# DRAM block sums shared out between the gate products and attention's first ten heads, with a new order in the opening and in attention's fill

## The chip, the cores and the metric

The kernel runs on one NeuronCore of a Trainium2 chip. The metric is the device time of one execution in microseconds (us). A NeuronCore has five engines that work side by side: TensorE (PE in the profile, with the loads of its stationary operand shown as PEld), VectorE (DVE), ScalarE (ACT), GpSimd (POOL) and SyncE (SP). Each works through its own instructions strictly in the order in which they were written, and waits where an operand isn't there yet. Data moves between DRAM and the on-chip memory by DMA; here three engines issue transfers: SP most of the loads, ACT the stores of results, POOL the transfers that add into their target.

## The reference, cut to what matters

One layer of a bidirectional encoder on 512 tokens of width 2048, all in float32:

```
h = rmsnorm(x) * norm_w
u = h @ w_in        # gate z | x,B,C | dt fwd | dt bwd | q-compress | kv-compress + rope key | attention gate | two branch gates
dt = softplus(dt + bias);  a = -exp(a_log);  da = dt * a
y = ssd(forward) + ssd(backward) + d_skip * x;  y = grouped rmsnorm(y * silu(z))
q, k, v from the compressed parts, rope on 64 of 192 columns, 16 heads
o = softmax(q k^T * scale) v * silu(attention gate)
out = rmsnorm(x + (sigmoid(g1) * (y @ w_proj_ssm) + sigmoid(g2) * (o @ w_proj_attn)) @ w_out)
```

## The kernel before, in words

**Numbers.** Every float32 product is made of three matmuls: each operand is split into a high part `h` and a rest `l` (32-bit words that TensorE takes at one column a step), and the product is wh·xh + wh·xl + wl·xh. A weight block comes by DMA into a raw buffer (`wraw`, three of them), ACT casts it to `wh` (L163, L433), DVE subtracts to get `wl` (L164, L434); `wh` and `wl` have three buffers each.

**Stages, in order of time.**

- *Opening.* `x` is loaded in eight blocks of 128 tokens by 1024 columns, ACT squares and sums each (L210), DVE and ACT make the reciprocal root (L185 to L191), `x` is scaled (L218 on ACT, L220 on DVE), TensorE transposes it (L225) and ACT and DVE write the parts `h_h` and `h_l` (L229, L230). The first product, `dtp` (dt and the rope key), starts after the last transpose. Its two weight blocks are split with the subtraction on POOL, all later ones on DVE.
- *x, B, C of group 0* (`xbc`), with the sums of h that later products need (L758 to L778) and softplus of dt (`dt_make`, L282 to L302) on DVE beside it.
- *Gates.* Three products of 2048 x 2048 by a Strassen scheme with seven smaller ones (P1, P5, P6, P2, P3, P7, P4), for each of two column halves `cp`; each small one is four blocks of weights, 48 matmuls. During P1 and P3 a second weight block is added onto the first by DMA on POOL's queue (`w_more`, L506), four times each, for use in the next product.
- *SSD.* Four groups of scans, with `xbc`, `qkv` and `za` products as fill between the steps.
- *Attention.* 16 heads. Per head four tiles of scores, softmax on DVE and ACT, transposes (L1348) and the product with v. Between them stand parts of the products that later heads need: rope queries (`t`), values (`vp`, L1265), queries and keys (`qp`, `kp`), taken from a queue called `fill` at the rate `unit` (L1494). `fill.until` forces what a head needs just before it.
- *Two output projections* (`wps`, `wpa`, again Strassen) *and the last one* (`wo`).

**Sums in DRAM.** For `wps` and `wpa` the added blocks T1 and T3 are made ahead in DRAM: 32 copies of 512 KB (L485) and 32 transfers that add to them (L486), all on POOL's queue, ordered so that each add comes two jobs after its copy. `in_background(n)` issues the next n of them. In the kernel before it is called once per head, behind the softmax of the second tile: four jobs in each of heads 0 to 7, six from head 8 until the 64 are used up.

**What sets the order.** TensorE's order is that of the program text. On the other engines a scheduler orders the instructions by its own estimates; `tc.high_priority(offset)` pulls what it encloses forward, and `keep_in_program_order` pins an instruction.

Of the kernel before, what the change touches and what calls it, by code (L numbers as in the profile page):

```python
# [18 lines left out]
P = 128  # L19
D = 2048  # L20
# [52 lines left out]
def build(tc, a):  # L73
# [83 lines left out]
    def wchunk(src, n):  # L157
        with tc.high_priority(offset=ahead[0]):
            raw = wp.tile([P, 1024], F32, tag="wraw", bufs=3, name="wraw")[:, :n]
            nc.sync.dma_start(raw, src)  # L160
            h = wp.tile([P, 1024], F32R, tag="wh", bufs=3, name="wh")[:, :n]
            l = wp.tile([P, 1024], F32R, tag="wl", bufs=3, name="wl")[:, :n]
            act.copy(h, raw)  # L163
            (dve if ahead[0] else pool).tensor_sub(l, raw, h.bitcast(F32))  # L164
        return h, l
# [37 lines left out]
    for t in range(TT):  # L203
        xt = xp.tile([P, D], F32, name=f"xt{t}")
        ss = few(2)
        for i in range(2):
            cs = slice(i * D // 2, (i + 1) * D // 2)
            nc.sync.dma_start(xt[:, cs], a["x"][t * P:(t + 1) * P, cs])
            scr = xp.tile([P, D // 2], F32, tag="scr", bufs=1, name="scr")
            act.activation(scr, xt[:, cs], AF.Square, accum_out=ss[:, i:i + 1])  # L210
        v = few(1)
        dve.tensor_add(v, ss[:, 0:1], ss[:, 1:2])
        dve.tensor_scalar(v, v, 1.0 / D, EPS, ALU.mult, ALU.add)
        r = small_rsqrt(v, 1, lambda n: few(1))
        for i in range(2):
            cs = slice(i * D // 2, (i + 1) * D // 2)
            if t >= TT - 2 and i == 1:
                act.activation(xt[:, cs], xt[:, cs], AF.Copy, scale=r)  # L218
            else:
                dve.tensor_scalar_mul(xt[:, cs], xt[:, cs], r)  # L220
        xs_t.append(xt)
    tps = [mm(), mm(), mm(), pa(), pa(), pb(), pb(), pc()]

    def x_turn(k, t):
        pe.transpose(tps[k % 8][:, t * P:(t + 1) * P], xs_t[t][:, k * P:(k + 1) * P], ident)  # L225

    def x_out(k):
        nw = vec[:, V_NORM + k:V_NORM + k + 1]
        act.activation(h_h[:, k, :], tps[k % 8], AF.Copy, scale=nw)  # L229
        dve.scalar_tensor_tensor(h_l[:, k, :], tps[k % 8], nw, h_h[:, k, :].bitcast(F32), ALU.mult, ALU.subtract)  # L230
# [12 lines left out]
    close_pool("xp")

    def win(tile_i):
        return [(a["wi"][tile_i, 0], 0, 8), (a["wi"][tile_i, 1], 8, 8)]

    def in_gemm(tile_i, n="mm"):
        return gemm(mm(n), win(tile_i), h_h, h_l)


# [17 lines left out]

    dtp = in_gemm(T_DT, "dtp")  # L270
    ahead[0] = AHEAD
    da_d = dr.tile([64, SEQ], F32, name="da_d")
    dv_, dt64 = sxd("dv_"), sxd("dt64")
    act.activation(dv_[0:64, :], dtp[0:64, :], AF.Identity, bias=vec[0:64, V_DTB:V_DTB + 1])
    act.copy(dv_[64:128, :], dtp[64:128, :])
    put(kr_d, dv_[64:128, :])

    def dt_make(new):

        v = dv_[0:64, :]  # L280
        e, u, pl, da64 = (new(n)[0:64, :] for n in ("e", "u", "pl", "da64"))
        dve.scalar_tensor_tensor(e, v, -1.0, v, ALU.mult, ALU.min)  # L282
        act.activation(e, e, AF.Exp)
        an = few(1)[0:64, :]
        tc.keep_in_program_order(act.activation(an, vec[0:64, V_ALOG:V_ALOG + 1], AF.Exp))
# [9 lines left out]
        dve.scalar_tensor_tensor(dt64[0:64, :], pl, 2.0, v, ALU.mult, ALU.add)  # L295
        dve.tensor_scalar_mul(an, an, -1.0)
        dve.tensor_scalar_mul(da64, dt64[0:64, :], an)
        act.copy(dt64[64:128, :], da64)
        act.dma_start(da_d[0:NH, :], da64[0:NH, :])
        chunked = lambda t: t[NH:64, :].rearrange("p (c l) -> p c l", c=TT)  # L300
        dve.tensor_mul(chunked(pl), chunked(dt64)[:, :, ::-1], an[NH:64, :].unsqueeze(2).broadcast_to([NH, TT, P]))
        act.dma_start(da_d[NH:64, :], pl[NH:64, :])  # L302
        put(dt_d, dt64)

# [96 lines left out]
    def za_gen(i):  # L401
        p_ = mm("za")
        yield from gemm_steps(p_, win(T_ZA + i), h_h, h_l)
        g_ = st("za")
        act.activation(g_, p_, AF.Silu)
        put(za_d[i], g_)
# [464 lines left out]
    vneg = few(8)  # L871
    dve.tensor_scalar_mul(vneg, vec[:, V_SN + 8:V_SN + 16], -1.0)

# [377 lines left out]
    def v_gen(hg):  # L1251

        v_h = at.tile([P, TT, SEQ], F32R, tag="v_h", bufs=2, name="v_h")
        v_l = at.tile([P, TT, SEQ], F32R, tag="v_l", bufs=2, name="v_l")
        vs[hg] = (v_h, v_l)
        for i in range(2):
            wh, wl = wchunk(a["wv"][hg, i], 1024)
            for t2 in range(2):
                vp = mm("vp")
                for t in (2 * t2, 2 * t2 + 1):  # L1260
                    o = vp[:, (t % 2) * 256:(t % 2 + 1) * 256]
                    tk = slice(t * P, (t + 1) * P)
                    for k in range(4):
                        s_ = slice(k * 256, (k + 1) * 256)
                        pe.matmul(o, ckv_h[:, k, tk], wh[:, s_], start=(k == 0), stop=False)  # L1265
                        pe.matmul(o, ckv_h[:, k, tk], wl[:, s_], start=False, stop=False)
                        pe.matmul(o, ckv_l[:, k, tk], wh[:, s_], start=False, stop=(k == 3))
                        yield 1.5
                vv = vp.rearrange("p (t c) -> p t c", t=2)
                sl = (slice(None), slice(2 * t2, 2 * t2 + 2), slice(i * 256, (i + 1) * 256))  # L1270
                act.copy(v_h[sl], vv)
                dve.tensor_sub(v_l[sl], vv, v_h[sl].bitcast(F32))
            yield None

# [30 lines left out]
    rv = chain(rope_gen(0), v_gen(0))  # L1305
    for i in range(4):
        fill.add("rv", part(rv))
    fill.add(("qk", 0), qk_gen(0))
    for hd in range(1, AH):
        fill.add(("qk", hd), qk_gen(hd))  # L1310
        if hd % 4 == 1 and hd < 12:
            rv = chain(rope_gen(hd // 4 + 1), v_gen(hd // 4 + 1))
        if hd < 12 and hd % 4:
            for _ in range(2 if hd % 4 == 3 else 1):
                fill.add(("rv", hd), part(rv))
    fill.until(("qk", 0))
# [5 lines left out]
    def scores(hd, t):  # L1322
# [433 lines left out]
def layout(inp):  # L1756
# [4 lines left out]
    for g in range(GROUPS):  # L1761
# [14 lines left out]
    wk = c(ukv[:, :, :, :P].transpose(2, 1, 0, 3))  # L1776
    wv = c(ukv[:, :, :, P:].reshape(4, P, 4, 2, 256).transpose(2, 3, 1, 0, 4))
    f = np.float32
# [6 lines left out]
        np.concatenate([inp["dt_bias_fwd"][0], inp["dt_bias_bwd"][0], z64])[:, None],  # L1785
        np.concatenate([inp["a_log_fwd"][0], inp["a_log_bwd"][0], z64])[:, None]], axis=1)
    i = np.arange(P)
# [25 lines left out]
```

## Time and profile before

| what | us |
|---|---|
| median of three runs | 2008.22 (2007.54 to 2011.87) |
| the profiled execution | 2010.63 |
| its span, first to last instruction | 2008.8 |
| PE busy | 1941.0 |
| DVE busy | 1481.6 |
| ACT busy | 1032.3 |
| POOL busy | 250.1 |

The profiled execution's own time is 1.8 us above its span and 2.4 us above the median of the runs. A line of groups reads: line, engine, operation, output<-inputs, shapes, count, then busy time and the mean of one in ns, then the idle time before them and what ended it. A matmul's duration in such a line runs until its results have left the array, so successive ones overlap; how often one starts is read from the start times in the timeline. The line of a window gives its bounds, its length, busy time (and count) of each engine, the share of full clock that TensorE was granted (PEclk), the share of time in which the DMA engines were busy, and GB/s.

### The profile page before, as it was taken

The page shows a single profiled execution, that of the slowest core. Times are in us where ns is not written, and L with a number is a line of the kernel's source. Part 1 is how long each engine was busy: PE and PEld are TensorE (multiplying, and loading weights), DVE is VectorE, ACT ScalarE, POOL GpSimd, SP SyncE. Part 2 cuts the span into 40 slices and gives each one's busy share as a digit, 9 for nine tenths or more (in the row PEclk, how much of TensorE's full clock was granted, in tenths as well). Part 3 has the DMA queues.
Part 4 walks back from the last instruction along what each step waited for, and adds up shares of the span by engine and source line. Part 5 has one row for each costly group of instructions (what it writes and reads, how often), then busy time and mean ns, then how long its engine had stood idle before and what let it go on. Part 6 is the DMA issues. An engine that isn't in the chain of part 4 may idle for free.

```text
span 2008.8 us, 24843 instructions
## 1 busy us (share of the span) xinstructions
PE 1941.0 (97%) x9026; PEld 1606.9 (80%) x9026; DVE 1481.6 (74%) x2064; ACT 1032.3 (51%) x1527; POOL 250.1 (12%) x315
## 2 busy tenths in 40 slices
PE   6999999999999999999999999999979999999997
PEld 4888888888878878887878788888867787888886
DVE  7976676676659879798794767666666898879466
ACT  6444445444464757757666344444444455444243
POOL 0001001001012020120200101112112111100011
PEclk9999999999999999999999999999989999999998
DMA  5468558558444635665454956877998687857446
GB/s 189 163 192 215 152 131 220 139 134 226 130 153 142 194 122 164 213 187 181 151 173 137 271 153 177 223 202 220 236 254 297 213 290 283 277 169 242 163 88 158
DMA packets 168907, 382.78 MB, mean 191 GB/s; under 512 B 16272, under 2 KB 65552, under 8 KB 168592
## 3 DMA queue, kind: packets, MB, share of 16 engines
q1 hardware_dynamic: 103248, 233.61, 35.3%
q0 software_dynamic: 30656, 103.30, 23.3%
q10 hardware_dynamic: 34880, 44.28, 6.2%
q8 instruction: 71, 1.16, 0.2%
q14 instruction: 52, 0.43, 0.1%
HBM read 329.22 MB, written 98.04 MB: 213 GB/s over the span
## 4 chain that ended last, share of the span: by engine, by line
PE 75%; DVE 10%; DMA 8%; issue 3%; ACT 3%; POOL 0%; SPq 0%; ACTq 0%; DVEq 0%; POOLq 0%
PE P L580 11%; PE P L581 11%; PE P L579 11%; PE xbc L168 3%; PE xbc L169 3%; PE xbc L170 3%; DMA wraw<-wps 2%; PE za L170 2%; PE za L168 2%; PE za L169 2%; PE qkv L168 1%; PE qkv L170 1%; PE qkv L169 1%; PE f L1582 1%; PE f L1581 1%
## 5 line engine op out<-in xcount | busy, mean ns | idle before, releaser
L433 ACT CAST wh<-X 128x1024 fp32r<-128x1024 f32 x164 | 172.9, 1056 | 198.4 <-PE P L581 152.2
L434 DVE TENSOR_TENSOR wl<-X,wh 128x1024 fp32r<-128x1024 f32 x164 | 200.1, 1224 | 91.2 <-ACT wh L433 90.8
L164 DVE TENSOR_TENSOR wl<-wraw,wh 128x1024 fp32r<-128x1024 f32 (+2 forms) x148 | 172.6, 1167 | 91.6 <-ACT wh L163 86.1
L163 ACT CAST wh<-wraw 128x1024 fp32r<-128x1024 f32 (+2 forms) x150 | 145.1, 970 | 120.3 <-PE xbc L169 37.7
L434 DVE TENSOR_TENSOR wl<-Y,wh 128x1024 fp32r<-128x1024 f32 x88 | 107.6, 1224 | 69.7 <-ACT wh L433 69.6
L168 PE MATMUL xbc<-h_h,wh 128*128 128x512 f32 x384 | 153.3, 399 | 0.0
L433 ACT CAST wh<-Y 128x1024 fp32r<-128x1024 f32 x88 | 92.8, 1056 | 115.9 <-PE P L581 105.8
L170 PE MATMUL xbc<-h_h,wl 128*128 128x512 f32 x384 | 150.3, 391 | 0.0
L169 PE MATMUL xbc<-h_l,wh 128*128 128x512 f32 x384 | 150.1, 391 | 0.0
L579 PE MATMUL P<-wh,h_h 128*128 128x512 f32 x384 | 149.4, 389 | 0.0
L580 PE MATMUL P<-wl,h_h 128*128 128x512 f32 x384 | 149.4, 389 | 0.0
L581 PE MATMUL P<-wh,h_l 128*128 128x512 f32 x384 | 149.4, 389 | 0.0
L433 ACT CAST wh<-wraw 128x1024 fp32r<-128x1024 f32 x68 | 71.8, 1055 | 120.4 <-PE P L581 63.5
L434 DVE TENSOR_TENSOR wl<-wraw,wh 128x1024 fp32r<-128x1024 f32 x68 | 83.2, 1224 | 66.5 <-ACT wh L433 66.5
L580 PE MATMUL P<-wl,S 128*128 128x512 f32 x288 | 112.3, 390 | 0.5 <-DVE wl L434 0.5
L579 PE MATMUL P<-wh,S 128*128 128x512 f32 x288 | 112.1, 389 | 0.0
L581 PE MATMUL P<-wh,S 128*128 128x512 f32 x288 | 112.1, 389 | 0.0
L170 PE MATMUL za<-h_h,wl 128*128 128x512 f32 x256 | 100.1, 391 | 2.0 <-DVE wl L164 2.0
L168 PE MATMUL za<-h_h,wh 128*128 128x512 f32 x256 | 101.6, 397 | 0.0
L169 PE MATMUL za<-h_l,wh 128*128 128x512 f32 x256 | 99.7, 389 | 0.0
L1335 ACT ACTIVATE pr<-s,nm 128x512 f32<-128x512 f32 x64 | 44.2, 690 | 82.9 <-DVE nm L1333 82.2
L170 PEld LDWEIGHTS xbc<-h_h,wl 128*128 128x128 f32 x384 | 72.3, 188 | 15.6
(748 smaller groups left out, 5188.6 us busy)
## 6 DMA issues: line engine op xcount, KB each, us to landing
wraw<-wi SPq DMA_DIRECT2D x102, 512.0 KB, 3.7
da<-da_d SPq DMA_DIRECT2D x64, 256.0 KB, 4.1
T_wps<-wps POOLq DMA_DIRECT2D x32, 512.0 KB, 9.5
T_wpa<-wpa POOLq DMA_DIRECT2D x32, 512.0 KB, 11.4
wraw<-wps SPq DMA_DIRECT2D x24, 512.0 KB, 6.7
wraw<-wo SPq DMA_DIRECT2D x20, 512.0 KB, 3.5
xbc_d<-xbc ACTq DMA_DIRECT2D x24, 256.0 KB, 2.3
wraw<-wun SPq DMA_DIRECT2D x16, 384.0 KB, 6.1
```

The costliest lines, as they stand in the source:

```text
L163: act.copy(h, raw)
L164: (dve if ahead[0] else pool).tensor_sub(l, raw, h.bitcast(F32))
L168: pe.matmul(out, wh, xh, start=start, stop=False)
L169: pe.matmul(out, wh, xl, start=False, stop=False)
L170: pe.matmul(out, wl, xh, start=False, stop=stop)
L433: i = act.copy(hi_, raw)
L434: dve.tensor_sub(lo_, raw, hi_.bitcast(F32))
L579: pe.matmul(bs[i], xh, wh, start=(j == 0), stop=False)
L580: pe.matmul(bs[i], xh, wl, start=False, stop=False)
L581: pe.matmul(bs[i], xl, wh, start=False, stop=(j == 7))
L1335: act.activation(pr, s, AF.Exp, bias=nm, scale=SCALE, accum_out=sm_)
L1581: pe.matmul(acc, mh, wl, start=False, stop=False)
```

## The change

In words:

- *Opening.* `x`'s last block comes in two halves of 512 columns; `vec` and most of `cst` are loaded behind `x`, and from SP. The root is taken by ACT straight from the accumulated squares (the earlier parts come in as its bias), and DVE's refinement has one instruction less. The scaling of the third token block moves from ACT to DVE. Both blocks of dt weights are subtracted on DVE. Seven banks, not eight, turn in the transposes; the eighth belongs to `dtp` from the start, whose matmuls stand between the transposes, seven steps behind.
- *dt.* Softplus runs on 128 partitions by 256 columns where it had 64 by 512; the second half of the tokens is moved to the upper partitions by a DMA. There are eight stores where there were three.
- *Gates.* Each of the six halves calls `in_background(2)` after P1 and after P3: 24 jobs. Attention then has 40 left, four in each of heads 0 to 9, and none later.
- *Values.* `v_gen` multiplies all 512 columns at once where it had 256 (the weights are laid out anew for it): 192 matmuls for 384. Both weight blocks are split before the first of them.
- *Attention's fill.* `unit` is 2.95 (was 2.77), falling to 2.4 and 1.7 near the end; the forced part now counts against what is owed; rope and value parts stand at other heads.
- *za.* The SiLU that empties a `za` bank has priority.

**Where instructions move.** POOL's queue in the gates, `wz` first (X and Y are the adds of `w_more`, T the sums in DRAM). Before:

```order
L506 DMA X<-wz 128x1024 x4
L506 DMA Y<-wz 128x1024 x4
L506 DMA X<-wz 128x1024 x4
L506 DMA Y<-wz 128x1024 x4
L506 DMA X<-wgs 128x1024 x4
L506 DMA Y<-wgs 128x1024 x4
```

With the change:

```order
L530 DMA X<-wz 128x1024 x4
L509 DMA T_wps_199<-wps 128x1024 x2
L530 DMA Y<-wz 128x1024 x4
L509 DMA T_wps_199<-wps 128x1024
L510 DMA T_wps_199<-wps 128x1024
L530 DMA X<-wz 128x1024 x4
L509 DMA T_wps_199<-wps 128x1024
L510 DMA T_wps_199<-wps 128x1024
L530 DMA Y<-wz 128x1024 x4
```

Two jobs stand behind each set of four adds and ahead of the next set.

ACT at the end of the opening, from the seventh block of squares on (`xt_288` and `xt_284` are the last token block). Before:

```order
L210 ACTIVATE scr,small<-xt_288 128x1024
L218 ACTIVATE xt_271<-xt_271,small 128x1024
L210 ACTIVATE scr,small<-xt_288 128x1024
L163 CAST wh<-wraw 128x1024
L185 ACTIVATE small<-small 128x1
L163 CAST wh<-wraw 128x1024
L218 ACTIVATE xt_288<-xt_288,small 128x1024
```

With the change:

```order
L209 ACTIVATE scr,small<-xt_284 128x1024
L209 ACTIVATE scr,small<-xt_284 128x512 x2
L215 ACTIVATE small<-small 128x1
L223 ACTIVATE xt_284<-xt_284,small 128x1024
L162 CAST wh<-wraw 128x1024
L239 ACTIVATE h_h<-mm,vec 128x512 x3
```

The casts of the weights have moved behind the root, and the scaling of another token block is gone from between the squares.

PE at the start of head 8, from the last matmuls of its keys (`kp`) to its first scores (`s`). Before:

```order
L168 MATMUL kp<-ckv_h,wh 128x512
L169 MATMUL kp<-ckv_l,wh 128x512
L170 MATMUL kp<-ckv_h,wl 128x512
L1326 MATMUL s<-kh,qh 128x512
L1327 MATMUL s<-kl,qh 128x512
```

With the change, around the same scores (the last `kp` of this head stands 101 rows earlier):

```order
L167 MATMUL qp<-cq_h,wh 128x512
L168 MATMUL qp<-cq_l,wh 128x512
L169 MATMUL qp<-cq_h,wl 128x512
L1348 MATMUL s<-kh,qh 128x512
L1349 MATMUL s<-kl,qh 128x512
```

Before, the scores follow the keys at once (heads 8 and 12; ten matmuls lie between in head 4); now at least 24 matmuls and transposes lie between in every head.

The diff, cut to its core:

```diff
-    act.dma_start(cst, a["cst"])
-    act.dma_start(vec, a["vec"])
+    act.dma_start(cst[:, :P], a["cst"][:, :P])
...
             act.copy(h, raw)
-            (dve if ahead[0] else pool).tensor_sub(l, raw, h.bitcast(F32))
+            dve.tensor_sub(l, raw, h.bitcast(F32))
...
+        edges = (0, 1024, 2048) if t < TT - 1 else (0, 1024, 1536, 2048)
+        for i, cs in enumerate(slice(*e) for e in zip(edges, edges[1:])):
             nc.sync.dma_start(xt[:, cs], a["x"][t * P:(t + 1) * P, cs])
...
+        act.activation(root, ss[:, i:i + 1], AF.Sqrt, bias=most, scale=1.0 / D)
+        dve.tensor_scalar(v, ss[:, i:i + 1], 1.0 / D, most, ALU.mult, ALU.add)
+        dve.reciprocal(r, root)
+        dve.scalar_tensor_tensor(root, r, r, v, ALU.mult, ALU.mult)
+        dve.tensor_scalar(root, root, -0.5, 1.5, ALU.mult, ALU.add)
+        dve.tensor_mul(r, r, root)
...
+    BANKS = (mm, mm, mm, pa, pa, pb, pb)
+    dtp, dt_w = pc("dtp"), []
+    def dt_mm(k):
+        h, l = dt_w[k // 8]
+        cs = slice(k % 8 * P, (k % 8 + 1) * P)
+        mm3(dtp, h[:, cs], l[:, cs], h_h[:, k, :], h_l[:, k, :], k == 0, k == KT - 1)
...
+    for k in range(7, KT):
+        for t in range(TT):
+            x_turn(k, t)
+        x_out(k)
+        if k == 10:
+            dt_w.append(wchunk(a["wi"][T_DT, 1], 1024))
+        dt_mm(k - 7)
+    for k in range(KT - 7, KT):
+        dt_mm(k)
...
-        v = dv_[0:64, :]
-        e, u, pl, da64 = (new(n)[0:64, :] for n in ("e", "u", "pl", "da64"))
+        v, dt2 = vd[:, 0:HS], vd[:, HS:SEQ]
+        e, u, pl, da2 = (new(n)[:, 0:HS] for n in ("e", "u", "pl", "da2"))
...
-        act.activation(g_, p_, AF.Silu)
+        with tc.high_priority(offset=ahead[0]):
+            act.activation(g_, p_, AF.Silu)
         put(za_d[i], g_)
...
+    for g_ in gates:
+        for cp in range(2):
+            for name in ("P1", "P3"):
+                g_.hooks.setdefault((cp, name), []).append(lambda: in_background(2))
...
-        for i in range(2):
-            wh, wl = wchunk(a["wv"][hg, i], 1024)
...
+        ws = [wchunk(a["wv"][hg, i], 1024) for i in range(2)]
+        for t in range(TT):
+            vp = mm("vp")
+            for k in range(4):
+                wh, wl = (w[:, k % 2 * SEQ:(k % 2 + 1) * SEQ] for w in ws[k // 2])
+                pe.matmul(vp, ckv_h[:, k, tk], wh, start=(k == 0), stop=False)
+                pe.matmul(vp, ckv_h[:, k, tk], wl, start=False, stop=False)
+                pe.matmul(vp, ckv_l[:, k, tk], wh, start=False, stop=(k == 3))
...
-            in_background(4 if hd < 8 else 6)
+            in_background(4)
...
-        fill.until(("qk", hd))
-        unit = 2.77 if hd < AH - 2 else 2
+        while ("qk", hd) not in fill.done:
+            owed[0] -= fill.step()
+        unit = 2.95 if hd < AH - 5 else 2.4 if hd < AH - 3 else 1.7 if hd < AH - 2 else 2
```

More of the change, by code (lines that the diff above doesn't have):

```diff
@@ L204, in build @@
         xt = xp.tile([P, D], F32, name=f"xt{t}")
-        ss = few(2)
-        for i in range(2):
-            cs = slice(i * D // 2, (i + 1) * D // 2)
+        edges = (0, 1024, 2048) if t < TT - 1 else (0, 1024, 1536, 2048)
+        ss = few(3)
+        for i, cs in enumerate(slice(*e) for e in zip(edges, edges[1:])):
             nc.sync.dma_start(xt[:, cs], a["x"][t * P:(t + 1) * P, cs])
-            scr = xp.tile([P, D // 2], F32, tag="scr", bufs=1, name="scr")
+            scr = xp.tile([P, D // 2], F32, tag="scr", bufs=1, name="scr")[:, :cs.stop - cs.start]
@@ L210, in build @@
             act.activation(scr, xt[:, cs], AF.Square, accum_out=ss[:, i:i + 1])
[L211 to L220, printed above, removed]
+            if i == 0:
+                most, v, root, r = (few(1) for _ in range(4))
+                dve.tensor_scalar(most, ss[:, 0:1], 1.0 / D, EPS, ALU.mult, ALU.add)
+            elif i < len(edges) - 2:
+                dve.tensor_scalar(most, ss[:, i:i + 1], 1.0 / D, most, ALU.mult, ALU.add)
@@ new lines, in build @@
+        act.activation(root, ss[:, i:i + 1], AF.Sqrt, bias=most, scale=1.0 / D)
[4 more added lines that the diff above has]
+        dve.tensor_mul(r, r, root)
+        dve.tensor_scalar_mul(xt[:, 0:1024], xt[:, 0:1024], r)
+        if t == TT - 1:
+            act.activation(xt[:, 1024:], xt[:, 1024:], AF.Copy, scale=r)
+        else:
+            dve.tensor_scalar_mul(xt[:, 1024:], xt[:, 1024:], r)
@@ L221, in build @@
         xs_t.append(xt)
-    tps = [mm(), mm(), mm(), pa(), pa(), pb(), pb(), pc()]
+    nc.sync.dma_start(vec, a["vec"])
+    BANKS = (mm, mm, mm, pa, pa, pb, pb)
+    tps = {}
     def x_turn(k, t):
-        pe.transpose(tps[k % 8][:, t * P:(t + 1) * P], xs_t[t][:, k * P:(k + 1) * P], ident)
+        if k not in tps:
+            tps[k] = BANKS[k % 7]()
+        pe.transpose(tps[k][:, t * P:(t + 1) * P], xs_t[t][:, k * P:(k + 1) * P], ident)
     def x_out(k):
         nw = vec[:, V_NORM + k:V_NORM + k + 1]
-        act.activation(h_h[:, k, :], tps[k % 8], AF.Copy, scale=nw)
-        dve.scalar_tensor_tensor(h_l[:, k, :], tps[k % 8], nw, h_h[:, k, :].bitcast(F32), ALU.mult, ALU.subtract)
+        act.activation(h_h[:, k, :], tps[k], AF.Copy, scale=nw)
+        dve.scalar_tensor_tensor(h_l[:, k, :], tps[k], nw, h_h[:, k, :].bitcast(F32), ALU.mult, ALU.subtract)
@@ L232, in build @@
+    dtp, dt_w = pc("dtp"), []
[3 more added lines that the diff above has]
+        mm3(dtp, h[:, cs], l[:, cs], h_h[:, k, :], h_l[:, k, :], k == 0, k == KT - 1)
     for t in range(TT - 1):
-        for k in range(8):
+        for k in range(7):
             x_turn(k, t)
-    for k in range(8):
+    dt_w.append(wchunk(a["wi"][T_DT, 0], 1024))
+    nc.sync.dma_start(cst[:, P:], a["cst"][:, P:])
+    for k in range(7):
         x_turn(k, TT - 1)
@@ L246, in win @@
         return [(a["wi"][tile_i, 0], 0, 8), (a["wi"][tile_i, 1], 8, 8)]
-    def in_gemm(tile_i, n="mm"):
-        return gemm(mm(n), win(tile_i), h_h, h_l)
     sx = open_pool("sx", reuse_waits="tile")
@@ L268, in put @@
         act.dma_start(dst, t)
-    dtp = in_gemm(T_DT, "dtp")
     ahead[0] = AHEAD
     da_d = dr.tile([64, SEQ], F32, name="da_d")
-    dv_, dt64 = sxd("dv_"), sxd("dt64")
-    act.activation(dv_[0:64, :], dtp[0:64, :], AF.Identity, bias=vec[0:64, V_DTB:V_DTB + 1])
+    HS = SEQ // 2
+    vd, dv_ = sxd("vd"), sxd("dv_")
+    for o, cs in ((vd, slice(0, HS)), (dv_, slice(HS, SEQ))):
+        act.activation(o[0:64, 0:HS], dtp[0:64, cs], AF.Identity, bias=vec[0:64, V_DTB:V_DTB + 1])
     act.copy(dv_[64:128, :], dtp[64:128, :])
+    act.dma_start(vd[64:128, 0:HS], dv_[0:64, 0:HS])
     put(kr_d, dv_[64:128, :])
     def dt_make(new):
-        v = dv_[0:64, :]
-        e, u, pl, da64 = (new(n)[0:64, :] for n in ("e", "u", "pl", "da64"))
+        v, dt2 = vd[:, 0:HS], vd[:, HS:SEQ]
+        e, u, pl, da2 = (new(n)[:, 0:HS] for n in ("e", "u", "pl", "da2"))
         dve.scalar_tensor_tensor(e, v, -1.0, v, ALU.mult, ALU.min)
         act.activation(e, e, AF.Exp)
-        an = few(1)[0:64, :]
-        tc.keep_in_program_order(act.activation(an, vec[0:64, V_ALOG:V_ALOG + 1], AF.Exp))
+        an = few(1)
+        tc.keep_in_program_order(act.activation(an, vec[:, V_ALOG:V_ALOG + 1], AF.Exp))
         dve.tensor_scalar(u, e, 2.0, None, ALU.add)
@@ L871, in build @@
     vneg = few(8)
-    dve.tensor_scalar_mul(vneg, vec[:, V_SN + 8:V_SN + 16], -1.0)
+    tc.keep_in_program_order(dve.tensor_scalar_mul(vneg, vec[:, V_SN + 8:V_SN + 16], -1.0))
     def add_fill(kind, n):
@@ L1255, in v_gen @@
         vs[hg] = (v_h, v_l)
-        for i in range(2):
-            wh, wl = wchunk(a["wv"][hg, i], 1024)
[L1258 to L1273, printed above, removed]
+        ws = [wchunk(a["wv"][hg, i], 1024) for i in range(2)]
+        for t in range(TT):
+            vp = mm("vp")
+            tk = slice(t * P, (t + 1) * P)
+            for k in range(4):
[3 more added lines that the diff above has]
+                pe.matmul(vp, ckv_l[:, k, tk], wh, start=False, stop=(k == 3))
+                yield 3
+            act.copy(v_h[:, t], vp)
+            dve.tensor_sub(v_l[:, t], vp, v_h[:, t].bitcast(F32))
+        yield None
     def qk_gen(hd):
@@ L1305, in build @@
     rv = chain(rope_gen(0), v_gen(0))
-    for i in range(4):
+    for i in range(3):
         fill.add("rv", part(rv))
@@ L1310, in build @@
         fill.add(("qk", hd), qk_gen(hd))
-        if hd % 4 == 1 and hd < 12:
+        if hd % 4 == 2 and hd < 12:
             rv = chain(rope_gen(hd // 4 + 1), v_gen(hd // 4 + 1))
-        if hd < 12 and hd % 4:
-            for _ in range(2 if hd % 4 == 3 else 1):
-                fill.add(("rv", hd), part(rv))
+        if hd % 4 != 1 and hd <= 12:
+            fill.add(("rv", hd), part(rv))
     fill.until(("qk", 0))
@@ L1776, in layout @@
     wk = c(ukv[:, :, :, :P].transpose(2, 1, 0, 3))
-    wv = c(ukv[:, :, :, P:].reshape(4, P, 4, 2, 256).transpose(2, 3, 1, 0, 4))
+    wv = c(ukv[:, :, :, P:].reshape(2, 2, P, 4, 512).transpose(3, 0, 2, 1, 4))
     f = np.float32
@@ L1785, in layout @@
         np.concatenate([inp["dt_bias_fwd"][0], inp["dt_bias_bwd"][0], z64])[:, None],
-        np.concatenate([inp["a_log_fwd"][0], inp["a_log_bwd"][0], z64])[:, None]], axis=1)
+        np.concatenate([inp["a_log_fwd"][0], inp["a_log_bwd"][0]] * 2)[:, None]], axis=1)
     i = np.arange(P)
```

22 lines of the change are left out of this document (10 added, 12 removed).

## The prediction, made before the changed kernel ran

> **What bounds the kernel now.** I read the busy shares first, then TensorE's waits, then a window or the chain of waits around each.
>
> ```profile
> PE 1941.0 (97%) x9026; PEld 1606.9 (80%) x9026; DVE 1481.6 (74%) x2064; ACT 1032.3 (51%) x1527; POOL 250.1 (12%) x315
> ...
> PE mm L225 <- DVE xt L220: 19.8, 4, 11.6
> ...
> PE pb L1348 <- DVE pr L1337: 10.0, 2, 6.3
> ...
> PE vp L1265 <- ACT za L405: 2.7, 1, 2.7
> ...
> PE s L1326 <- ACT kh L1283: 2.5, 2, 1.2
> ...
> PE s L1327 <- DVE kl L1284: 1.9, 3, 0.7
> ```
>
> A wait row gives the total, the times and the longest, in us. TensorE is the bound: an edit counts only if it shortens TensorE's list or takes away one of its waits. The waits are few and sit in four places (opening, values, some heads' scores, attention's end), and the change touches all four. What else it does lies in the gates, where TensorE hardly waits: that is where it can lose.
>
> **The opening: 5.5 us (2 to 8).** ACT, POOL, DVE and PE:
>
> ```profile
> 16.57 1.15 ACT L218 ACTIVATE xt<-xt,small 128x1024 f32<-128x1024 f32 x1
> 18.58 0.19 ACT L210 ACTIVATION_READ_ACCUMULATOR scr<-xt 128x1 f32 x1
> ...
> 19.78 4.64 POOL L164 TENSOR_TENSOR wl<-wraw,wh 128x1024 fp32r<-128x1024 f32 x2 [18.90 <-ACT wh L163]
> ...
> 12.89 0.16 DVE L188 TENSOR_TENSOR small<-small 128x1 f32<-128x1 f32 x1
> 20.04 2.10 DVE L188 TENSOR_TENSOR small<-small 128x1 f32<-128x1 f32 x1
> 22.17 2.27 DVE L189 TENSOR_TENSOR small<-small 128x1 f32<-128x1 f32 x1
> ...
> 26.90 2.07 DVE L230 SCALAR_TENSOR_TENSOR h_l<-mm,vec,h_h 128x512 fp32r<-128x512 f32 x3 [1.29 <-ACT h_h L229]
> ...
> 25.66 0.90 PE L225 MATMUL mm<-cst,xt 128*128 128x128 f32 x3 [6.32 <-DVE xt L220]
> 32.97 0.50 PE L168 MATMUL dtp<-h_h,wh 128*128 128x512 f32 x1
> ...
> 44.15 0.23 PE xbc L168
> ```
>
> The last block's squares end at 18.77, and from there to TensorE's first transpose of it pass 6.89 us. 4.05 of them are two one-column DVE instructions that take 2.10 and 2.27 us where the same line took 0.16: they run exactly while POOL subtracts. With the subtractions on DVE and behind the root, that goes. The scaling (1.15) leaves ACT's list between the squares, and the root needs no step on DVE ahead of it: some 2 us of ACT's path in all. So the squares end near 16.7; a root (0.2) and five DVE steps of 0.2 give the factor at 17.9, and the first transpose follows at about 18.7, 7.0 us earlier.
>
> Part of that is given back. Before, every matmul of dtp ran in one stretch from 32.97 to 44.15. Now DVE sets the pace: behind the first transpose come a scaling, a cast and a subtraction on ACT and DVE (some 3 us), so h_l starts near 22; then 16 h_l of 0.69 (2.07 for three) and three more subtractions of 1.22 (row below) are 14.7, to 36.7; with some hand-overs and the last dtp matmuls I get 38.6 for the first xbc matmul, 5.5 earlier. The upper end, 8, is the 7.0 and one hand-over less. The lower end, 2, is this gain taken back at the first gate, whose X blocks wait for adding transfers:
>
> ```profile
> 117.28 1.06 ACT L433 CAST wh<-X 128x1024 fp32r<-128x1024 f32 x1 [4.03 <-DMA X<-wz]
> 127.18 3.08 ACT L433 CAST wh<-X 128x1024 fp32r<-128x1024 f32 x3 [2.12 <-DMA X<-wz]
> ...
> 44.10:98.70 54.60, 54.60 (x243) 45.21 (x242) 53.28 (x60) 27.23 (x32) 0.00 (x0) 1.00 0.47 150
> ```
>
> The last of them lands at 127.18; if it stays there while TensorE comes 5.5 earlier, what TensorE has in hand there (about 2 us by these rows) decides. I expect it to move along, since its start hangs on SP's list, which moves too. The window shows what could still spoil it: beside xbc DVE is busy for 53.28 of 54.60 us, so it has no room for more. dt on 128x256 has half the columns for each of its DVE steps, which leaves room; its extra transfer and five more stores lie beside 54 us of TensorE's work. I count neither; without that cover the transfer would cost about the 3.7 us that one of 512 KB takes (row further down).
>
> **Values: 2.6 us (0 to 4).** Four starts in the second half of v_gen and behind it:
>
> ```profile
> 1166.30 0.28 PE L1267 MATMUL vp<-wh,ckv_l 128*128 128x256 f32 x1
> 1173.85 0.28 PE L1267 MATMUL vp<-wh,ckv_l 128*128 128x256 f32 x1
> 1175.13 0.39 PE L170 MATMUL qp<-cq_h,wl 128*128 128x512 f32 x1
> 1179.89 0.39 PE L170 MATMUL kp<-ckv_h,wl 128*128 128x512 f32 x1
> ```
>
> A duration holds the time until the results are out, so I go by starts. The first two rows lie 63 matmuls apart: 7.55/63 = 0.120 us each at 256 columns; the last two 21 apart: 4.76/21 = 0.227 at 512. 384 x 0.120 = 46.1 against 192 x 0.227 = 43.5. [...]
>
> **Keys: 4.4 us (2 to 5.5).** The five waits for kh and kl (2.5 + 1.9) stand where the keys are made directly ahead of the scores. With 24 or more matmuls between, 24 x 0.227 = 5.4 us cover ACT's and DVE's steps of about a microsecond each. Lower end: two of the three heads still meet a late kl, because DVE has something else first.
>
> **za: 3.5 us (0 to 7.5).**
>
> ```profile
> 1157.76 1.26 ACT L1212 CAST kra<-o 32x512 fp32r<-32x512 f32 x2
> 1159.05 0.60 ACT L405 ACTIVATE za<-za 128x512 f32<-128x512 f32 x1
> ...
> 1158.97:1165.80 6.83, 6.11 (x28) 6.11 (x29) 6.62 (x11) 4.00 (x7) 0.54 (x1) 0.50 0.76 223
> ```
>
> TensorE waits for a bank that za's SiLU empties, and the SiLU stands behind the casts of kra. The granted clock is then 0.50 for 6.83 us, which costs half of the 6.11 busy, 3.1. In the change's order the SiLU stands ahead of the second pair of casts, 1.3 us earlier. A wait of 1.4 instead of 2.7 would probably leave the clock alone: 1.3 + 3.1 = 4.4; if not, 1.3. I take 3.5; the bounds are nothing, and wait and clock with a hand-over, 7.5. [...]
>
> **Attention's end: 11 us (3 to 13).** The chain of waits, two windows, and the transfers of 1400 to 1500 (KB each, median us to landing):
>
> ```profile
> 1457.96 9.11 DMA wraw<-wps
> 1469.49 5.34 DMA wraw<-wps
> ...
> 1486.60 10.73 DMA wraw<-wps
> ...
> 1498.43 1.22 DVE wl L434
> ```
>
> ```profile
> 1479.80:1483.20 3.40, 2.95 (x9) 2.58 (x10) 2.84 (x6) 3.25 (x5) 3.04 (x6) 0.50 0.86 136
> 1496.90:1503.70 6.80, 2.81 (x9) 2.45 (x10) 5.08 (x10) 4.48 (x8) 1.38 (x2) 0.50 1.02 254
> ```
>
> ```profile
> T_wpa<-wpa POOLq DMA_DIRECT2D x20, 512.0 KB, 12.5
> wraw<-wps SPq DMA_DIRECT2D x6, 512.0 KB, 7.9
> ...
> wraw<-wi SPq DMA_DIRECT2D x102, 512.0 KB, 3.7
> ```
>
> TensorE waits 10.0 us for pr, which is ready late because DVE and ACT hold, in order, a cast and a subtraction for a weight block that is still in flight. A block of 512 KB takes 5 to 11 us here and 3.7 at its median elsewhere, with the DMA engines full (1.02). Half of the busy time in the two half-clock stretches, (2.95 + 2.81)/2 = 2.9, comes on top: 12.9. In this stretch 20 of the sums are under way; the change has none after head 9. I take 11, since the wps and yn_x loads themselves stay; at the low end only the smaller of the two waits (10.0 - 6.3 = 3.7, less a hand-over) goes. The other edits of the fill move TensorE's work and change nothing of its amount; they cost nothing as long as every tile of scores keeps some matmuls to run while pr is made. Where it doesn't, the wait for pr comes back, which is the first rival.
>
> **The gates: -1 us (-6 to 0).** After P1 the DMA engines are idle, after P3 they are full; then the loads of X and the cast that needs them:
>
> ```profile
> 199.65:202.38 2.73, 2.73 (x14) 2.26 (x13) 2.69 (x3) 1.06 (x1) 0.00 (x0) 1.00 0.00 0
> 237.87:240.60 2.73, 2.73 (x14) 2.26 (x13) 1.24 (x2) 1.06 (x1) 0.00 (x0) 1.00 0.97 168
> ...
> 248.95 8.48 SPq L469 DMA_DIRECT2D X<-wgs  x4
> 257.49 1.06 ACT L433 CAST wh<-X 128x1024 fp32r<-128x1024 f32 x1 [1.66 <-PE P L581]
> ...
> X<-wgs SPq DMA_DIRECT2D x4, 512.0 KB, 4.5
> ```
>
> A job is a 512 KB transfer on POOL's queue, behind the adds already there and ahead of the next. Its price I take from the first gate: three adds lay between the casts of 117.28 and 127.18, 3.3 us each, so 6.6 for a hook's two. Against that stands: X is issued at 248.95, there at 253.5, and its cast at 257.49 waited for TensorE, not for data: 4 us; and three buffers of wh let TensorE run on for two blocks (2 x 2.73) once casts are late. That makes 9.4 us, more than 6.6. The six hooks after P1 meet an idle DMA. So about nothing; I take 1, and for the low end one us for each of the six hooks after P3. If the cover were gone, each would cost its 6.6.
>
> **Sum.** 5.5 + 2.6 + 4.4 + 3.5 + 11 - 1 = 26. The profiled execution took 2010.63, so 1984.6; it lies 2.4 above the median of the runs, so 1982.
>
> **Rivals.**
>
> - *The end of attention stalls as before* (chance 0.14). For it: the wps and yn_x loads stay, and a fill that runs out earlier puts TensorE sooner in front of pr. Against it: 20 sums fewer in 100 us. It takes the 11 away: 1993.
> - *The gates give it back* (0.04). At each of the six hooks after P3 two thirds of the price, 4.2 of 6.6, come through: 25. With 26 gained that leaves 1: 2007, no change. Against: the 9.4 us.
> - *Slower: P3 hooks fully exposed* (0.04). The jobs stand ahead of adds on a full DMA system, so X comes two jobs later and the cover counts for nothing, because Y and X queue behind each other: 6 x 6.6 = 40 lost against 27 gained, 2008 + 13 = 2021. It decides from 4.5 us lost at each hook after P3, that is from a delay of about 14 us. [...]
> - *More than forecast* (0.06). Attention's many small losses shrink as well, since its DMA load falls everywhere: 20 us more, 1962. By the durations 0.28 and 0.39 alone, values would save 33 us; the starts speak against it.
> - *Forecast*: 0.72.
>
> **Range and chances.** The terms' own bounds, added as independent, give some 12 down and 11 up; the first rival widens the upper side: 1970 to 1997. Left out are the gate rivals (0.08), half of the last, and tails. A measurement of this kernel tells about 0.2% (4 us) from no change. Faster takes the forecast, the first and the last rival and what of the second falls below 2004: 0.93; same 0.03; slower 0.04.
>
> **What would show it.** First xbc matmul near 38.6, DVE's one-column steps at 0.16 everywhere; vp starts 0.227 apart; no wait of s for kh or kl; granted clock 1.00 around vp and up to the end of attention; wraw<-wps landing in 4 to 5 us and no pr wait of several us; in the gates no wait of P for wl beyond a microsecond. Waits of wh for X or Y after P3 of several us would make it wrong, as would waits of pb for pr spread over all heads, or a first gate that starts no earlier.

## The result and the profile after

| | before | after |
|---|---|---|
| median of four runs, us | 2008.7 (2007.5 to 2011.9) | 1986.96 (1985.1 to 1988.1) |
| ratio | | 0.989, 95% interval 0.9874 to 0.9906 |
| span of the profiled execution | 2008.8 | 1985.8 |

The change is 21.7 us faster by the medians and 23.0 by the spans; 26 were forecast. The busy line and the chief waits of TensorE, after:

```profile
span 1985.8 us, 24464 instructions
...
PE 1933.5 (97%) x8834; PEld 1593.3 (80%) x8834; DVE 1476.5 (74%) x2064; ACT 1029.3 (52%) x1527; POOL 246.3 (12%) x309
...
PE mm L235 <- DVE xt L221: 13.0, 4, 9.4
PE P L604 <- DVE wl L458: 6.6, 8, 1.5
PE pb L1370 <- DVE pr L1359: 4.7, 1, 4.7
...
PE vp L1290 <- ACT za L429: 1.4, 1, 1.4
...
PE vp L1291 <- DVE wl L163: 1.0, 2, 0.8
```

The waits of scores for kh and kl are gone. Those for za (2.7 before) and pr (10.0) are halved, not gone. A wait of vp for wl is new.

The waits don't tell it all, because the clock drops after some of them (0.50 for 6.83 us at the values, before and after). So I took the start times of all TensorE instructions from the timeline. For each pair of neighbours, what lies between two starts beyond the instruction's own step (0.227 us at 512 columns, 0.120 at 256) is lost time. It is put to the pair, named by the tiles that the two write; what the slow steps inside half-clock windows lose is summed by itself. Landmarks and losses, before and after, in us:

| stretch | before | after | gain |
|---|---|---|---|
| first xbc matmul | 44.15 | 38.00 | 6.2 |
| from there through the gates | | | -0.8 |
| SSD, up to the first rope matmul `t` | | | 0.0 |
| first `t` to last `op` | 382.2 | 365.3 | 16.9 |
| of it: steps of the value matmuls | 46.1 | 43.6 | 2.5 |
| value matmul to value matmul | 0.6 | 3.8 | -3.2 |
| keys to scores, scores to scores, `op` to `op` | 10.3 | 2.1 | 8.2 |
| `t` to the first value matmul (za) | 2.9 | 1.5 | 1.4 |
| into the transposes `pb` from other work | 11.5 | 5.0 | 6.5 |
| half clock | 5.2 | 3.2 | 2.0 |
| all other pairs | | | -0.5 |
| after the last `op` | | | 0.8 |

The opening after, in the chain of waits and in the timeline:

```profile
37.77 0.23 PE dtp L169
38.00 0.23 PE xbc L167
```

```profile
16.78 0.22 DVE L218 SCALAR_TENSOR_TENSOR small<-small 128x1 f32<-128x1 f32 x1
17.03 0.15 DVE L219 TENSOR_SCALAR small<-small 128x1 f32<-128x1 f32 x1
...
18.22 0.90 PE L235 MATMUL mm<-cst,xt 128*128 128x128 f32 x3 [1.30 <-DVE xt L221]
```

The one-column steps of DVE take about 0.2 us where two had taken 2.1 and 2.3. The transposes of the last token block start at 18.22 (18.7 forecast), the first xbc matmul at 38.00 (38.6).

The end of attention in the chain of waits, after:

```profile
1469.22 6.19 DMA wraw<-wps
1475.48 1.05 ACT wh L457
1476.56 1.23 DVE wl L458
1477.78 0.41 DVE pr L1359
1478.33 0.95 PE pb L1370 x4
```

The transfers of the same blocks from 1440 to 1500 (median us to landing last):

```profile
wraw<-wps SPq DMA_DIRECT2D x10, 512.0 KB, 5.1
```

One block of wps weights is still late. The softmax waits behind its subtraction as before, but once where it was twice.

### The profile page after: what moved, and what is told of

Same layout as the page of the kernel before. It is cut to its first block, busy times and chain, and to the rows that moved or that the text cites. A ratio compares the mean times of both kernels' runs of the same rounds, so it can differ in the third digit from the quotient of the medians.

```text
span 1985.8 us, 24464 instructions
## 1 busy us (share of the span) xinstructions
PE 1933.5 (97%) x8834; PEld 1593.3 (80%) x8834; DVE 1476.5 (74%) x2064; ACT 1029.3 (52%) x1527; POOL 246.3 (12%) x309
## 3 DMA queue, kind: packets, MB, share of 16 engines
q0 software_dynamic: 30656, 103.30, 22.9%
## 4 chain that ended last, share of the span: by engine, by line
PE 79%; DVE 9%; DMA 5%; issue 4%; ACT 2%; POOL 1%; SPq 0%; ACTq 0%; DVEq 0%; POOLq 0%
PE P L604 11%; PE P L605 11%; PE P L603 11%; PE xbc L167 4%; PE xbc L168 4%; PE xbc L169 4%; PE za L169 2%; PE za L167 2%; PE za L168 2%; DVE sum L1098 2%; PE qkv L167 1%; PE qkv L169 1%; PE f L1603 1%; PE f L1604 1%; PE qkv L168 1%
## 5 line engine op out<-in xcount | busy, mean ns | idle before, releaser
L603 PEld LDWEIGHTS P<-wh,h_h 128*128 128x128 f32 x384 | 72.1, 188 | 15.0
## 6 DMA issues: line engine op xcount, KB each, us to landing
T_wps<-wps POOLq DMA_DIRECT2D x32, 512.0 KB, 10.8
```

The lines of the kernel that those rows point to most:

```text
L603: pe.matmul(bs[i], xh, wh, start=(j == 0), stop=False)
```

## The experiments

Ratios are to the kernel before on the same chip. The runs stand on several chips, and one ratio is good to about 0.2% (4 us), so a difference of 2 or 3 us between two experiments is inside the noise of the times; what is said of it rests on the traces, one profile for each kernel. "Stretch" is the time from the first `t` to the last `op`, 382.2 before and 365.3 in the change.

**The sums as before, all else as in the change.**

```diff
-    for g_ in gates:
-        for cp in range(2):
-            for name in ("P1", "P3"):
-                g_.hooks.setdefault((cp, name), []).append(lambda: in_background(2))
...
-            in_background(4)
+            in_background(4 if hd < 8 else 6)
```

> The changed kernel with the sums in DRAM as before: none in the gates, four in each of heads 0 to 7, six from head 8 on. Theory 1 (the sums' transfers are what made the weight blocks late at attention's end): 1992 to 1998 us, that is 5 to 11 slower than the change; wraw<-wps takes 8 us or more to land again, and the waits of pb for pr come to 9 us or more. Rival (the new fill cured the end by giving TensorE more to do there): 1985 to 1989, waits of pb for pr about 5 as in the change. The first gate should lose nothing (last product of the gates 6.2 us earlier than before, 5.35 in the change) if the sums in the gates cost the 0.8 us seen there; 5.35 again if the opening's own lead ran into the adds.

1990.9 us, ratio 0.9912 (0.9884 to 0.994); stretch 369.1. The time lies between what the two accounts gave, 1 us below theory 1 and 2 above the rival; the trace decides. A wait row and a row of transfers of 1440 to 1500:

```profile
PE pb L1366 <- DVE pr L1355: 12.2, 2, 10.0
```

```profile
wraw<-wps SPq DMA_DIRECT2D x9, 512.0 KB, 6.6
...
T_wpa<-wpa POOLq DMA_DIRECT2D x2, 512.0 KB, 12.6
```

The waits for pr are back at 12.2 us with the new fill in place, so the fill alone did not cure them. In time the sums are worth less here than alone: about 4 us, and the intervals of this kernel and of the change overlap. From the first scores on they are worth 6.9, but this execution kept the full clock at the values, where the change's profile lost it. The blocks landed in 6.6 us rather than the 8 I expected (5.1 in the change). The last gate product came 5.24 us earlier than before against 5.37 for the first xbc: the lead is kept without sums in the gates.

**The sums moved, all else as before.** The same two edits in the other direction.

> The kernel before with only the sums moved (24 to the gates, 40 in heads 0 to 9). Theory 1: the waits of pb for pr shrink from 10.9 us to 5 or less and the half clock with them: 1999 to 2003 us. Rival: unchanged, 2006 to 2011. By either, the gates lose 0 to 1 us: last gate matmul at 567 to 568.

1996.8 us, ratio 0.9944 (0.9926 to 0.9961); stretch 369.2, 13.0 less. The waits:

```profile
PE pb L1352 <- DVE pr L1341: 2.4, 3, 1.0
```

From 10.0 to 2.4 us, and no half clock at attention's end. From the first scores on the gain is 10.7 us, which is the 11 of the prediction; the rest is one half-clock window fewer at the values and the SSD's scatter. The gates lose 0.1. Theory 1 holds, and by more than I gave it (1999 to 2003).

**The fill's order and rates, all else as before** (values 256 wide, in one part).

```diff
-        fill.until(("qk", hd))
-        unit = 2.77 if hd < AH - 2 else 2
+        while ("qk", hd) not in fill.done:
+            owed[0] -= fill.step()
+        unit = 2.95 if hd < AH - 5 else 2.4 if hd < AH - 3 else 1.7 if hd < AH - 2 else 2
...
-        if hd < 12 and hd % 4:
-            for _ in range(2 if hd % 4 == 3 else 1):
-                fill.add(("rv", hd), part(rv))
+        if hd % 4 != 1 and hd <= 12:
+            fill.add(("rv", hd), part(rv))
```

> The kernel before with only the new order and rates of attention's fill (values stay 256 wide). Theory 1: the waits of s for kh and kl go (about 6 us by start times) and the end of attention stays as it was, waits of pb for pr 9 us or more: 2001 to 2004 us. Rival (the fill cures the end too): 1993 to 1997.

1998.1 us, ratio 0.9951 (0.993 to 0.9972); stretch 371.4. TensorE has no wait of s for kh or kl any more, and:

```profile
PE pb L1347 <- DVE pr L1336: 10.4, 2, 8.3
```

The end stalls as before, so the rival falls, though the median lies between the two accounts; this profile is the slowest of its seven executions (1993.9 to 2002.7). The gain from the first scores on is 8.7 us, not 6: besides the two gaps ahead of the scores (2.8), the lost time between scores falls from 5.6 to 2.3 and between `op` matmuls from 1.8 to nothing.

**The opening and dt, all else as before.** The diff's first two parts.

> The kernel before with only the new opening and dt on 128x256. Both theories: first xbc matmul at 37.8 instead of 44.0, and 2001 to 2004 us. If the 0.8 us lost at the first gate come from the sums there, the lead is still 6.2 us at the last product of the gates; if the first gate's X blocks can't follow the lead, it is 5.4 there without any sums in the gates.

2004.2 us, ratio 0.9977 (0.9961 to 0.9993), single executions from 1997.9 to 2008.6. First xbc 5.4 us earlier than before (6.2 expected), last gate product 5.3. So a lead of 5.4 passes the first gate. Over the nine kernels with the new opening and at most four sums behind a product, the lead at xbc is 5.1 to 6.2, and what the gates take of it is between -0.7 and 0.9, with the 0.8 of the change at the upper end; no part of the change goes with that.

**The last za product pinned ahead of sine and cosine**, in the change.

```diff
-    fill.run(36)
+    fill.all()
     dve.tensor_scalar(ang2, ang, math.pi / 2, None, ALU.add)
     wrap(ang)
-    act.activation(sinT, ang, AF.Sin)
+    tc.keep_in_program_order(act.activation(sinT, ang, AF.Sin))
     wrap(ang2)
-    act.activation(cosT, ang2, AF.Sin)
-
-    fill.run(48)
+    tc.keep_in_program_order(act.activation(cosT, ang2, AF.Sin))
```

> The changed kernel with the last za product issued ahead of the sine and cosine, and these two pinned behind its SiLU on ACT; that also moves the subtraction of the second block of value weights ahead of the rope work on DVE. Theory 1 (the clock fell at the values because TensorE stood idle for about half of the 3.4 us ahead of it, in two pieces of 1.5 and 0.5): no wait of vp for za, no half clock at 1154 to 1161, and 5 to 7 us faster than the change, 1980 to 1982. Rival (the clock falls there for another reason): the waits go, the half clock stays, 2 to 3 us faster, 1984 to 1985.

1984.05 us, ratio 0.9882 (0.9863 to 0.99): not clear of the change's 0.989 (0.9874 to 0.9906). A wait and two windows of this kernel:

```profile
PE vp L1288 <- DVE qb L1261: 2.7, 1, 2.7
```

```profile
1154.67:1158.09 3.42, 1.22 (x6) 0.68 (x4) 3.38 (x6) 2.01 (x4) 0.00 (x0) 1.00 0.58 134
1158.09:1161.50 3.41, 2.92 (x7) 2.35 (x8) 3.41 (x7) 1.09 (x2) 0.00 (x0) 0.50 0.60 216
```

The wait for za is gone and another took its place: vp's second bank is one that holds a rope product, and DVE reads it only once sine and cosine are there. The clock fell behind that one. So neither account was right as written, though the time is the rival's: pulling ACT's step forward moves the stall on to DVE.

**Values 256 columns at a time**, in the change (the old `v_gen` in one part).

> The changed kernel with values made 256 columns at a time again (three parts as in the change). Theory 1 (the 512 wide form saves 2.5 us of matmuls, and gives 3 us back, since it needs both weight blocks before its eighth matmul): within 1.5 us of the change, with waits of vp for wl of less than 1 us in place of 3.8. Rival (the saving of the prediction holds): 2.6 slower, 1989 to 1990.

1984.7 us, ratio 0.9883 (0.9866 to 0.9899), no slower than the change where the prediction's term would have it 2.6 us slower; stretch 362.0. The matmuls take 2.5 us more, and between value matmuls 1.4 us are lost instead of 3.8. Steps and losses of the values come to 47.5 us here and 47.4 in the change: the wide form is worth nothing either way. The shorter stretch has other reasons, one half-clock window fewer among them.

**Values 512 columns at a time, all else as before** (four parts).

```diff
+        ws = [wchunk(a["wv"][hg, i], 1024) for i in range(2)]
+        for t in range(TT):
...
+                pe.matmul(vp, ckv_h[:, k, tk], wh, start=(k == 0), stop=False)
+                pe.matmul(vp, ckv_h[:, k, tk], wl, start=False, stop=False)
+                pe.matmul(vp, ckv_l[:, k, tk], wh, start=False, stop=(k == 3))
...
+            if t % 2:
+                yield None
```

> The kernel before with only the values 512 columns at a time (four parts as before). The prediction's term: 2.6 us faster, 2005 to 2007. Theory 1 (2.5 us of matmuls saved, the wait for the second block's wl added): 2007.5 to 2010, with waits of vp for wl that the kernel before has not.

2012.2 us, ratio 1.0023 (1.0013 to 1.0032): slower by 4.7 us, outside what either account gave. A wait of TensorE, the transfer of rope weights (`wur`) in the chain that led to it, and ACT's steps:

```profile
PE s L1322 <- ACT kh L1279: 6.0, 2, 4.1
```

```profile
1335.48 11.26 DMA wraw<-wur
```

```profile
1346.84 0.83 ACT L163 CAST wh<-wraw 128x768 fp32r<-128x768 f32 x1 [4.47 <-DMA wraw<-wur]
1347.58 0.58 ACT L1279 CAST kh<-kp 128x512 fp32r<-128x512 f32 x1
```

The wide form holds both blocks of value weights at once. In the old fill order the next rope weights were then issued at 1335.48 (1330.91 before) and took 11.26 us to land, beside four of the sums; ACT stood 4.47 us in front of their cast, and the cast of kh behind it. The waits for kh grew from 2.5 to 6.0 us, more than the 2.5 of the matmuls.

**Four sums behind each P3, none behind P1**, and then **eight**, with the rest in the heads from head 0 on.

```diff
-            for name in ("P1", "P3"):
-                g_.hooks.setdefault((cp, name), []).append(lambda: in_background(2))
+            g_.hooks.setdefault((cp, "P3"), []).append(lambda: in_background(4))
```

> The changed kernel with all 24 sums of the gates behind P3, four for each, none behind P1. By the prediction's price (3.3 us for one, 13.2 for four) and cover (9.4 us): 3.8 us lost at each of six places, 23 in all, 2010. Rival (the price is much smaller than 3.3, since the DMA engines work on several transfers at once): 1986 to 1989, no wait of P for wl beyond 1 us in the gates.

> The changed kernel with 48 of the sums behind P3, eight for each, and 16 in heads 0 to 3. By the prediction's price and cover (26.4 against 9.4 us): 17 us lost at each of six places, about 100 in all. Theory 1 (POOL and the DMA engines have some 24 us between two sets of adds, in which eight sums pass): 1984 to 1992.

Four: 1987.95 us, ratio 0.9896 (0.9877 to 0.9915), no different from the change; the gates lose nothing (lead 5.7 at the first xbc matmul, 5.9 at their end). Eight: 2003.8 us, ratio 0.9975 (0.9958 to 0.9993); a lead of 4.7 turns into 16.2 behind: 20.9 us, 3.5 at each place, where I expected none or 17. ACT's waits for X blocks in the gates (116 to 585), before, with four, and with eight:

```profile
ACT wh L433 <- DMA X<-wz: 9.3, 4, 4.0
```

```profile
ACT wh L457 <- DMA X<-wga: 17.4, 10, 4.3
ACT wh L457 <- DMA X<-wgs: 14.8, 9, 4.2
ACT wh L457 <- DMA X<-wz: 5.0, 2, 3.2
```

```profile
ACT wh L457 <- DMA X<-wga: 32.0, 14, 6.6
ACT wh L457 <- DMA X<-wgs: 30.0, 15, 4.5
ACT wh L457 <- DMA X<-wz: 20.0, 9, 3.7
```

The mechanism of the slower rival exists: sums behind P3 make the X blocks late, 9 us of waits in all before, 37 with four, 82 with eight. With four the blocks in hand hide all of it. If the cover is the 9.4 us I worked out, which no run measures by itself, eight jobs that cost 3.5 beyond it take 12.9, which is 1.6 each, half of the 3.3 I had read off the first gate. Two jobs, as in the change, then take about 3 of the 9: ACT's waits for X come to 5.6 us there, all for wz, fewer than before.

**x12 loaded half a head later and split a tile and a half later**, in the change.

```diff
-        if hd == AH - 2:
-            y_ops.load("x12")
...
         if hd == AH - 1:
-            y_ops.split("x12", slot("x12"))
+            y_ops.load("x12")
...
         some(2 * unit)
+        if hd == AH - 1:
+            y_ops.split("x12", slot("x12"))
         scores(hd, 3)
```

> The changed kernel with the operand x12 of the first output projection loaded half a head later and split a tile and a half later, so that its two raw buffers are free for weight blocks meanwhile. Theory 1 (the 4.9 us left at attention's end come from weight blocks that wait for a raw buffer which an operand holds): the wait of pb for pr falls below 2 us and the half clock at 1478 goes, 3 to 5 us faster, 1982 to 1984. Rival (the stall is the landing time itself): 1986 to 1988.

1981.2 us (1979.4 to 1981.9), ratio 0.9863 (0.9847 to 0.9879), the lowest of all; stretch 358.8. SP's issues in the change, and then here:

```profile
1464.52 3.89 SPq L469 DMA_DIRECT2D xraw<-yn_x  x2
1469.22 0.33 SPq L493 DMA_DIRECT2D wraw<-wps  x1
```

```profile
1463.59 0.34 SPq L493 DMA_DIRECT2D wraw<-wps  x1
1467.15 1.46 SPq L469 DMA_DIRECT2D xraw<-yn_x  x2
```

In the change x12's two loads stand ahead of the weight block on SP, and the second waits for a raw buffer; weights and operands share three. Put behind it, the block leaves 5.6 us earlier. It lands 7.4 us earlier, the other 1.8 by a faster landing, though the blocks of wps take longer at the median (6.1 us, 5.1 in the change). The wait of pb for pr goes, one of 2.4 us for nm (made from the row maxima) is left, above the 2 us that theory 1 gave, and the half clock there goes. So theory 1 has the larger part of the mechanism. How much of the time is this edit's own stays open: of the 6.5 us that the stretch is shorter, 3.3 lie ahead of the first scores, where the edit changes nothing and the clock differs (last section), and 3.2 behind. From the first scores to the last `op` the three kernels with x12 later take 323.4 to 324.3 us; the change and four of the experiments on it that leave x12 alone take 323.4 to 328.6, where the lowest is the one with za pinned.

**x12 later and values 256 wide; then with za pinned as well.**

> The changed kernel with x12 later (as in the run before with that edit, 1981.2) and values 256 columns at a time (as in the run with that edit, 1984.7). Theory 1 (each takes away its own stall): the gains of 5.8 and 2.2 us add, 1977 to 1980. Rival (the gain of the narrow values was one window of half clock, that came or went with the phase of the windows): 1980 to 1982.

> The same with the last SiLU of za pinned ahead of sine and cosine. Theory 1 (the stall goes from za to the banks of the rope products, as it did in the run with that edit alone): no better than without the pin, within 1.5 us. Rival (with narrow values the banks are free in time): 2 to 4 us faster than without.

1984.65 us, ratio 0.9883 (0.9865 to 0.9901), and 1985.65, ratio 0.9888 (0.9872 to 0.9904). The first comes out above both of its accounts. Its stretch (358.9) equals that of x12 alone, so narrow values gave nothing there either, and after the stretch it has half-clock windows at 1530 and 1629 that x12 alone has not. So I do not know that the two edits add. The second is no better than the first, as theory 1 had it: the wait went on to the rope banks again (2.8 us between two value matmuls).

## Why the prediction was right, point by point

The sign was right, the size nearly (21.7 of 26), and the gates took almost nothing. Three of the four places gave their gain, the values with za less than 1 us. That the sum came so close is in part luck, since the errors of its terms offset each other: by the table the opening and the keys gave 4.5 us more than their terms, and values, za and the end 8 less.

- **Opening, 5.5: right**, 6.2 in this profile, 5.4 alone. DVE's one-column steps run at 0.15 to 0.22 us with POOL's subtractions gone; that these had been the cause fits both traces, but no run moved them alone. DVE's pace gave 38.6 for the first xbc matmul and 38.00 was measured.
- **Values, 2.6: failed.** The step that failed is taking the change in matmul steps (46.1 less 43.5) for the change in time. The steps were right, 2.5 us. What I left out is that the old form could start on one weight block, while the new one needs the second at its seventh matmul: 3.2 us came back between value matmuls. Undoing this part alone made the change no slower. Alone on the kernel before, it cost 4.7.
- **Keys, 4.4: right in mechanism, too small.** Alone 8.7, in the change 8.2. I counted the idle time of the five waits for kh and kl; by start times the same five cost 5.9. Another 1.8 lay between `op` matmuls. The wait rows put those gaps to nm and to the transposed parts of the softmax, not to the keys: the new fill took them away, and the prediction had no term for them.
- **za, 3.5: the wait right, the clock open.** The wait fell from 2.7 to 1.4 as worked out, but I had the clock stay up after 1.4 us of waiting. In this profile it fell, for the same 6.8 us (rows below). In the four experiments with the same wait and the wide values (sums as before, sums at P3 by four and by eight, x12 later) it stayed up, and from the first `t` to the first scores they take 35.1 to 35.6 us instead of 38.6. So the length of that wait alone did not tell the clock: the run with x12 later had it too, and other windows around it (last section).
- **Attention's end, 11: right in mechanism and alone (10.7), too large in the change**: 8.5 by the table (6.5 of waits and 2.0 of clock), 6.9 from the first scores on against the run with the sums as before, about 4 between the times of these two. The prediction kept 2 of the 12.9 back for the loads of wps and yn_x; what stayed is one block that stands behind an operand's loads on SP, and that order it did not see. The transfers did land sooner, in 5.1 us instead of 7.9.
- **The gates, -1: right in size**, -0.8 here and -0.1 alone. The price of 3.3 us for a job was too high, by half if the cover is the 9.4 us: 3.3 a job would have cost 17 us at each place with eight, and 3.5 was measured. It was read where three adds in a row stood, which may have waited for their own loads too. The cover was what decided, and it was there.
- Two of the signs did not come true: the clock fell at the values and once at the end of attention, and a pr wait of 4.7 us is left. The others did (vp starts, no wait for kh or kl, DVE's short steps, the gates).
- The SiLU's priority has no run of its own. The other four parts, each alone on the kernel before, give 12.1, 10.8, 4.7 and -4.7 us by the medians, 22.9 together; with 4 us of noise in each, that this is close to 21.7 shows little.
- The scatter I had no term for: the SSD part comes out between 1.7 us worse and 2.7 better from one profile to the next, in kernels whose code there is nearly the same.

## What to carry to other kernels

A transfer that nobody waits for can delay those that somebody does wait for: in the change the blocks of wps landed in 5.1 us at the median, with the sums put back as before in 6.6. Move it where the DMA engines stand idle, and check how much cover the consumers there have by doubling it.

A wider matmul saves steps, but asks for its operands sooner (2.5 us saved here, 3.2 lost). Count from which matmul on each operand is needed, before the steps are added up.

Where several users share raw buffers and one queue, look at the order of issue. In the change x12's second load stood on SP waiting for a buffer, and a weight block waited behind it; put ahead of it, the block left 5.6 us earlier.

## What the runs showed of the hardware

In the clock records of the two profiles, before and after, every stretch of one clock inside the kernel is a whole number of 3.41 us long: one or two of them at 0.50 (3.41 or 6.83 us), 4 to 261 at 1.00 (13.65 to 890.88). The steps of the clock lie on one grid in each profile, and the two grids have different phases (the records begin at 29.16 and 24.41 us, which is 1.85 and 0.51 past a multiple of 3.413). Windows of the change's profile, cut on its grid (PE's busy time is the first after the length; PEclk is third from the right):

```profile
1150.81:1154.22 3.41, 1.79 (x7) 1.05 (x6) 3.01 (x5) 3.31 (x6) 0.00 (x0) 1.00 0.25 80
1154.22:1157.64 3.42, 2.67 (x6) 1.38 (x5) 3.42 (x6) 1.27 (x2) 0.54 (x1) 0.50 0.89 299
1157.64:1161.05 3.41, 3.41 (x9) 2.67 (x9) 3.41 (x6) 1.65 (x3) 0.00 (x0) 0.50 0.43 144
...
911.88:915.29 3.41, 1.74 (x12) 1.29 (x11) 3.02 (x8) 2.51 (x7) 0.00 (x0) 1.00 0.69 230
915.29:918.71 3.42, 3.42 (x9) 2.63 (x8) 3.38 (x7) 3.42 (x7) 0.00 (x0) 0.50 0.11 32
573.96:577.38 3.42, 1.74 (x10) 1.53 (x11) 1.19 (x3) 3.11 (x7) 0.78 (x1) 1.00 0.59 233
577.38:580.79 3.41, 3.41 (x21) 2.83 (x20) 1.07 (x1) 3.11 (x7) 0.00 (x0) 1.00 0.00 0
```

Behind the windows in which TensorE was busy for 1.79 and 1.74 us of 3.41 came one at 0.50, although it was not idle for the whole window; behind another with 1.74 us (573.96) the clock stayed at 1.00. Counted by starts (0.227 us for each 512-column matmul, 0.120 at 256, 0.11 below), the shares are 36% and 43% in the two that were followed by half clock, 48% in the one that was not. Counted in the same way, each on its own grid and from the start of its clock record on, the profiles before and after hold seven windows at full clock with a share of 37% or less, and half clock followed all seven; of three between 43% and 45% it followed one, and of those above none.

A half-clock window full of matmuls costs some 1.7 us, half of its length (an estimate from the 0.50; starts of 512-column matmuls stand 0.43 us apart in it, 1158.23 and 1158.66, where they stand 0.227 apart at full clock). Behind the one in which TensorE was busy for 2.67 us of 3.42 (second row) the clock stayed at 0.50, behind the one with 3.41 (third row) it came back. The record of the clock begins at 24.4 us in this profile; ahead of that the view prints 1.00, while the starts of 512-column matmuls there are 0.43 us apart (22.81, 23.24), as in the half-clock windows.

The run with x12 later has the change's waits at the values (vp for za 1.4 us in both, for wl 1.3 us in all here and 1.0 there), but they fall into two windows in which TensorE was busy for 2.27 and 2.43 us, and the clock stayed at 1.00:

```profile
1149.37:1152.78 3.41, 2.27 (x11) 1.54 (x9) 2.98 (x6) 2.62 (x4) 0.00 (x0) 1.00 0.13 48
1152.78:1156.19 3.41, 2.43 (x7) 1.23 (x7) 3.37 (x5) 3.18 (x5) 0.54 (x1) 1.00 0.60 192
1156.19:1159.61 3.42, 2.70 (x12) 2.24 (x13) 3.42 (x6) 0.87 (x2) 0.00 (x0) 1.00 0.90 295
```

So by these profiles an edit that shortens a stall by 1 us could gain up to some 4 us (an estimate: the 1 us and two windows of 1.7) or nothing by the clock, depending on the phase. I take this to be a part of the few us by which single executions of one kernel differ; it was not tested.
